# Raw weights of the first four steps in eight large buffers, with the order of their splits and squares fixed

## The chip, the cores and the metric

The kernel runs on one core of a Trainium2 chip. The metric is the device time of one execution in microseconds; the time before is the median of three runs, 1448.05 us (1447.67 to 1449.76).

## The reference

One layer of a hybrid decoder works on 256 prompt tokens and 8 decode tokens (264 columns together), with a model width of 2048:

```python
x = x + concat([y_rg, y_ml]) @ w_out      # RG-LRU and mLSTM groups, fed by xn @ w_in, xn = rmsnorm(x)
x = x + cross_attention(rmsnorm(x), memory keys and values)
x = x + (silu(xf @ w_gate) * (xf @ w_up)) @ w_down      # xf = rmsnorm(x)
y = rmsnorm(x)
```

The part that matters here is the very first one: `xn @ w_in`, where `rmsnorm(x, g)` is `x * rsqrt(mean(x * x) + 1e-6) * g`. All arithmetic is float32.

## The kernel before

The kernel is a list of steps. A step loads a block of weights, splits it, multiplies it on TensorE with the activations and evacuates the sum. The activations lie with the model's width on the 128 partitions (16 blocks of 128 rows, held in the tile xres) and the 264 tokens along the row.

**Products of three.** TensorE multiplies in a reduced form, fp32r. To keep float32 accuracy each operand is cut into a head, which is the value rounded to fp32r, and a remainder, which is the value minus the head. A product takes three matmuls: head by head, head of the weights by remainder of the input, and remainder of the weights by head of the input (`mm3`). The heads are made by ScalarE, the remainders by VectorE, which needs the head first.

**The first four steps.** Steps 0 to 3 take the first 512 output columns of w_in. Step q covers the input blocks 4q to 4q + 3 and adds to four PSUM banks (`first`: three named ax, one named mm), so that work can start as soon as a little of x and of the weights has landed. I call one input block of a step, against 512 columns, a **chunk**: chunks 0 to 15, four to a step, each of twelve matmuls (four banks by three products). `load_first` loads a chunk's weights, 128 partitions by 4 runs of 128 elements, 256 KB in runs of 512 bytes; two chunks share a raw buffer (`raw_half`, five buffers in all). `load_x` loads blocks of xres, mostly in pairs. `split_first` makes, chunk by chunk, the input's head and remainder (`split`, with the gain g_mix), and the weights' head (ScalarE) and remainder (VectorE), in that order. From step 4 on a step has 1024 or 2048 weights a partition, split in halves of 1024 (`split_half`).

**The norm.** The rsqrt of the mean square is applied after the product, so only the sum of squares of x is needed, and not before the evacuation of step 3. Its sum is built in acc_x: blocks 0 to 7 by eight squares on ScalarE (`sumsq`) with seven additions on VectorE, behind step 1's code; blocks 8 to 15 by `last_squares`, two squares of 1056 columns and four additions, behind step 3's. In the middle of steps 5 and 6 TensorE sums acc_x over the partitions and spreads the result.

**What sets the order.** SyncE's queue, and ScalarE's and VectorE's rows of `split_first`, are in written order. The rest is placed by a scheduler by readiness and priority, so an instruction of a later step can be placed ahead of written-out rows. One such instruction matters here: the first line of `rg_coef`, a VectorE instruction of 8 columns that reads the RG-LRU's decay from the tile vecs. It belongs to work that begins at step 7. The tile vecs holds all small vectors; its first 16 columns (g_mix) are loaded by ScalarE's queue at the start, the other 442 columns by SyncE's queue behind the weights of step 1. Each engine works its own rows strictly in order. Eight semaphores (DMAHW0 to DMAHW7) mark landings in turn, so a transfer waits until the one eight places before it has landed.

In the views below one line, L61, stands for all computing instructions, since a helper records them; they are told apart by their tiles: `B<-xres,vecs` is an input's head or remainder, `w<-raw` a weights' head, `w<-raw,w` a weights' remainder, `t<-vecs` the line of rg_coef.

Of the kernel before, what the change touches and what calls it, by code (L numbers as in the profile page):

```python
# [17 lines left out]
P = 128  # L18
# [4 lines left out]
N = T + NS  # L23
# [72 lines left out]
def layer_kernel(ctx: ExitStack, tc, xT, memT, vec, wrg, w_in, w_out, w_q, w_k, w_v, w_o,  # L96
# [112 lines left out]
    def load_first(i, c):  # L209

        if c % 2 == 0:
            raws.setdefault(i, []).append(raw_half())
        r = raws[i][c // 2][:, c % 2 * 512: c % 2 * 512 + 512]
        sp.dma_start(r.rearrange("p (n m) -> p n m", m=P),
                     steps[i][0].rearrange("p (n c m) -> p c n m", c=4, m=P)[:, c])

    def split_first(i, h):

        wh, wl = wrows(sb.tile([P, WW], F32R, tag="w", bufs=4, name=nm("w")), i)
        r = raws[i][h].rearrange("p (c m) -> p c m", m=P)  # L220
        with tc.high_priority(), in_order():
            for c in range(2):
                x, k = 4 * i + 2 * h + c, slice(4 * c, 4 * c + 4)
                split(*xn(x), xres[:, x, :], V("g_mix", x))
                st["split"] = act.activation(wh[:, k], r[:, k], AF.Copy)
                dve.tensor_sub(wl[:, k], r[:, k], wh[:, k].bitcast(F32))
        splits[i, h] = (wh, wl)

    def last_squares():

        a, b = (B([P, BW])[:, 0: 4 * N] for _ in range(2))
        for t, q in ((a, 2), (b, 3)):
            act.activation(t, xres[:, 4 * q: 4 * q + 4, :].rearrange("p c n -> p (c n)"), AF.Square)
        dve.tensor_add(a, a, b)
        dve.tensor_add(a[:, 0: 2 * N], a[:, 0: 2 * N], a[:, 2 * N:])
        dve.tensor_add(a[:, 0: N], a[:, 0: N], a[:, N: 2 * N])
        dve.tensor_add(acc_x, acc_x, a[:, 0: N])
# [769 lines left out]
    def pe_first(q):  # L1007
        def f(i):
            w = W(i)
            for c in range(4):  # L1010
                for n in range(4):
                    mm3(first[n][:, :N], w(4 * c + n), rx(4 * q + c), q + c == 0, q + c == 6)
        return f
# [436 lines left out]
    for c in range(4):  # L1450
        load_first(0, c)
        if c == 0:
            load_x(sp, 1, 2)
        elif c == 1:
            load_x(sp, 2, 4)
# [7 lines left out]
    with tc.high_priority(), in_order():  # L1463
        load_x(act, 0, 1)
        act.dma_start(vecs[:, 0:16], vec[:, 0:16])
        act.activation(warm_act, ones[:, 0:1], AF.Square)
# [5 lines left out]
    kept = ExitStack()  # L1472
    for i, (src, cols, pef, evf, need) in enumerate(steps):
# [24 lines left out]
        if i == 4:  # L1498
            kept.enter_context(tc.manual_schedule(engines={mybir.EngineType.PE}))
# [3 lines left out]
        if i == 1:  # L1503
# [146 lines left out]
```

## Time and profile before

| | |
|---|---|
| median of three runs | 1448.05 us |
| the profiled execution | 1449.42 us |
| its span, from the first to the last instruction | 1447.7 us |
| TensorE busy | 1429.4 us (99%) |
| VectorE busy | 1050.5 us (73%) |
| ScalarE busy | 796.6 us (55%) |
| mean rate of all transfers | 227 GB/s |

The busy times are shares of the span. TensorE's matmuls are pipelined, so its busy time counts stretches in which it is fed, and its idle time is what the page shows as waits. Times inside the trace count from the first instruction. The 1.7 us between the execution and its span lie around the program.

### The profile page before, as it was taken

The numbers are of one execution on the slowest core, as the hardware profiler recorded it, in microseconds if no ns is written. First come the engines' busy times: TensorE is split into PE (matmuls) and PEld (weight loads), VectorE is DVE, ScalarE is ACT, GpSimd is POOL, SyncE is SP. The second block draws the span as 40 slices with busy tenths as digits, with TensorE's granted clock in tenths as the row PEclk, the third lists the DMA queues.
The fourth block names the chain that finished last, engine by engine and source line by source line (L and its number), as shares of the span: only waits on it lengthen the run. The fifth ranks groups of instructions, "written<-read, shape, count | busy, mean of one in ns | idle before, by whom it ended". The sixth has DMA issues, their size and how long they took to land.

```text
span 1447.7 us, 29974 instructions
## 1 busy us (share of the span) xinstructions
PE 1429.4 (99%) x11979; PEld 1405.0 (97%) x11979; DVE 1050.5 (73%) x2012; ACT 796.6 (55%) x1290; POOL 127.7 (9%) x203
## 2 busy tenths in 40 slices
PE   9999999999999999999999999999999999999997
PEld 8999999999999999899999999999999999999997
DVE  7966798998899999977675656555666655556565
ACT  7678786665556666655544444434444433444474
POOL 0001220000125433310000000000000000000000
PEclk9999999999999999999999999999999999999999
DMA  9745897557799887856555555555555555555473
GB/s 286 237 174 184 292 361 281 176 180 273 280 334 370 326 301 266 339 175 213 196 191 197 195 198 195 193 200 191 198 196 191 202 190 196 197 191 200 164 241 126
DMA packets 100764, 329.17 MB, mean 227 GB/s; under 512 B 11056, under 2 KB 19936, under 8 KB 100624
## 3 DMA queue, kind: packets, MB, share of 16 engines
q1 hardware_dynamic: 84624, 272.36, 54.0%
q0 software_dynamic: 15424, 54.22, 10.2%
q8 instruction: 93, 1.52, 0.4%
q10 hardware_dynamic: 576, 0.68, 0.1%
q14 instruction: 47, 0.39, 0.1%
HBM read 314.36 MB, written 12.86 MB: 226 GB/s over the span
## 4 chain that ended last, share of the span: by engine, by line
PE 56%; DVE 1%; issue 1%; ACT 0%; POOL 0%; DVEq 0%; POOLq 0%
PE mm L61 56%; DVE B L61 1%; PE ax L61 1%; DVE dw L61 0%; DVE w L61 0%; POOL ds L1198 0%; DVE t L61 0%; ACT dw L61 0%; ACT t L61 0%; DVE ax L61 0%; ACT ds L61 0%; ACT B L61 0%; ACT rstd L61 0%; DVEq L1627 0%; DVE xres L61 0%
## 5 line engine op out<-in xcount | busy, mean ns | idle before, releaser
L61 PE MATMUL mm<-B,w 128*128 128x264 f32 (+1 forms) x10960 | 1282.0, 279 | 1.8 <-DVE w L61 1.7
L61 PEld LDWEIGHTS mm<-B,w 128*128 128x128 f32 x10960 | 1261.3, 189 | 9.9 <-DVE w L61 2.3
L61 DVE TENSOR_TENSOR w<-raw,w 128x1024 fp32r<-128x1024 f32 (+1 forms) x522 | 624.0, 1197 | 300.4 <-ACT w L61 299.7
L61 ACT ACTIVATE w<-raw 128x1024 fp32r<-128x1024 f32 (+1 forms) x522 | 534.7, 1028 | 511.1 <-PE mm L61 350.8
L61 PE MATMUL mm<-w,B 128*128 128x512 f32 x384 | 86.9, 380 | 0.0
L61 PEld LDWEIGHTS mm<-w,B 128*128 128x128 f32 x384 | 70.6, 189 | 9.7 <-DVE w L61 0.4
L1540 POOL TENSOR_TENSOR B<-B,rstd 128x264 f32<-128x264 f32 x4 | 2.8, 748 | 801.1 <-ACT rstd L61 801.1
L61 DVE TENSOR_TENSOR t<-mm,rstd 128x264 f32<-128x264 f32 x96 | 41.4, 432 | 28.5 <-PE mm L61 28.4
L61 DVE SCALAR_TENSOR_TENSOR B<-B,dw 128x256 f32<-128x256 f32 x128 | 54.9, 481 | 3.1 <-ACT dw L61 3.0
L61 DVE TENSOR_TENSOR xres<-xres,mm 128x264 f32<-128x264 f32 (+1 forms) x81 | 34.1, 423 | 24.6 <-PE mm L61 24.6
L61 DVE SCALAR_TENSOR_TENSOR dw<-B,qsm,dw 128x256 f32<-128x256 f32 x96 | 48.4, 509 | 2.3 <-ACT dw L61 1.5
L61 PE MATMUL ax<-B,B 128*128 128x256 f32 (+3 forms) x276 | 44.6, 302 | 1.8 <-DVE B L61 1.0
L1198 POOL TENSOR_TENSOR ds<-dw,ds 128x256 fp32r<-128x256 f32 x32 | 35.4, 1105 | 106.8 <-ACT ds L61 106.6
L61 PEld LDWEIGHTS ax<-B,B 128*128 128x128 f32 x276 | 37.9, 191 | 4.5 <-DVE B L61 1.6
L61 ACT ACTIVATE B<-xres,vecs 128x264 fp32r<-128x264 f32 (+1 forms) x64 | 32.2, 503 | 4.0 <-DVE xres L61 2.7
L61 ACT ACTIVATE dw<-B,qsm 128x256 f32<-128x256 f32 x32 | 16.3, 508 | 27.0 <-issue 10.7
L1187 POOL DMA_DIRECT2D B<-kcT x32 | 17.3, 542 | 139.6 <-DVE B L61 126.5
L61 ACT ACTIVATE t<-xres 128x264 f32<-128x264 f32 (+1 forms) x53 | 21.1, 408 | 14.0 <-DVE xres L61 13.9
L61 ACT ACTIVATE dw<-B,B 128x128 f32<-128x128 f32 x64 | 21.2, 392 | 12.2 <-DMA B<-scr 9.0
L61 DVE SCALAR_TENSOR_TENSOR B<-xres,vecs,B 128x264 fp32r<-128x264 f32 x48 | 23.3, 486 | 4.0 <-ACT B L61 4.0
L61 ACT ACTIVATE dw<-ax,dw 128x256 f32<-128x256 f32 x32 | 15.0, 469 | 19.2 <-DVE dw L61 18.2
L61 ACT ACTIVATE B<-t 128x264 fp32r<-128x264 f32 (+1 forms) x60 | 24.1, 409 | 2.1 <-DVE t L61 2.1
(181 smaller groups left out, 680.3 us busy)
## 6 DMA issues: line engine op xcount, KB each, us to landing
raw<-w_gu SPq DMA_DIRECT2D x176, 512.0 KB, 4.1
raw<-w_d SPq DMA_DIRECT2D x80, 512.0 KB, 3.7
raw<-w_in SPq DMA_DIRECT2D x74, 512.0 KB, 5.1
raw<-w_out SPq DMA_DIRECT2D x32, 512.0 KB, 3.7
raw<-w_q SPq DMA_DIRECT2D x32, 512.0 KB, 5.5
B<-kcT POOLq DMA_DIRECT2D x32, 512.0 KB, 8.9
B<-vcT POOLq DMA_DIRECT2D x32, 512.0 KB, 10.4
raw<-w_k SPq DMA_DIRECT2D x32, 512.0 KB, 5.0
```

The source lines that it names most:

```text
L61: return f(*a, **k)
L1187: pool_e.dma_start(kc, kcT[h, b])
L1198: pool_e.tensor_sub(ws[:, 1], acc, ws[:, 0].bitcast(F32))
L1540: e.tensor_mul(st["y"](c), st["y"](c), r)
```

## The change

Five things are changed, all in steps 0 to 3:

1. The raw weights of these steps go to eight buffers of the large pool B instead of five shared ones, and from chunk 2 on two chunks come in one transfer of 512 KB, in runs of 1 KB. The input block 1 moves from SyncE's to ScalarE's queue.
2. VectorE, not ScalarE, makes the weights' head of chunk 0 (`tensor_copy`), ahead of the input's split.
3. The squares come in four equal batches of 1056 columns (`squares(q)`): batch 0 behind step 1's code, 1 behind step 2's, 2 and 3 behind step 3's.
4. ScalarE's and VectorE's rows are in written order from the start to the end of step 3's code (`early`), and not only inside `split_first`; TensorE's are in written order from the start to step 6 (`kept`), and not only from step 4.
5. The matmuls of chunk 0 are written product by product over the four banks.

```diff
     def load_first(i, c):
+        src = steps[i][0].rearrange("p (n c m) -> p n c m", c=4, m=P)
         if c % 2 == 0:
-            raws.setdefault(i, []).append(raw_half())
-        r = raws[i][c // 2][:, c % 2 * 512: c % 2 * 512 + 512]
-        sp.dma_start(r.rearrange("p (n m) -> p n m", m=P),
-                     steps[i][0].rearrange("p (n c m) -> p c n m", c=4, m=P)[:, c])
+            raws.setdefault(i, []).append(B([P, 1024]))
+        r = raws[i][c // 2].rearrange("p (n c m) -> p n c m", c=2, m=P)
+        if i + c // 2 == 0:
+            sp.dma_start(r[:, :, c], src[:, :, c])
+        elif c % 2:
+            sp.dma_start(r, src[:, :, c - 1: c + 1])
...
-        with tc.high_priority(), in_order():
+        with tc.high_priority():
             for c in range(2):
                 x, k = 4 * i + 2 * h + c, slice(4 * c, 4 * c + 4)
+                if x == 0:
+                    dve.tensor_copy(wh[:, k], r[:, :, c])
                 split(*xn(x), xres[:, x, :], V("g_mix", x))
-                st["split"] = act.activation(wh[:, k], r[:, k], AF.Copy)
-                dve.tensor_sub(wl[:, k], r[:, k], wh[:, k].bitcast(F32))
+                if x > 0:
+                    st["split"] = act.activation(wh[:, k], r[:, :, c], AF.Copy)
+                dve.tensor_sub(wl[:, k], r[:, :, c], wh[:, k].bitcast(F32))
...
-    def last_squares():
+    def squares(q):
-        a, b = (B([P, BW])[:, 0: 4 * N] for _ in range(2))
-        for t, q in ((a, 2), (b, 3)):
-            act.activation(t, xres[:, 4 * q: 4 * q + 4, :].rearrange("p c n -> p (c n)"), AF.Square)
-        dve.tensor_add(a, a, b)
...
+        t = B([P, BW])[:, 0: 4 * N]
+        act.activation(t, xres[:, 4 * q: 4 * q + 4, :].rearrange("p c n -> p (c n)"), AF.Square)
+        dve.tensor_add(t[:, 0: 2 * N], t[:, 0: 2 * N], t[:, 2 * N:])
+        if q == 0:
+            dve.tensor_add(acc_x, t[:, 0: N], t[:, N: 2 * N])
+            return
+        dve.tensor_add(t[:, 0: N], t[:, 0: N], t[:, N: 2 * N])
+        dve.tensor_add(acc_x, acc_x, t[:, 0: N])
...
+                if q + c == 0:
+                    for k, l in ((0, 0), (0, 1), (1, 0)):
+                        for n in range(4):
+                            pe.matmul(by2(first[n][:, :N]), w(n)[k], turn(rx(0)[l]), start=k + l == 0, stop=False)
+                    continue
...
-        if c == 0:
-            load_x(sp, 1, 2)
-        elif c == 1:
+        if c == 1:
             load_x(sp, 2, 4)
...
-    with tc.high_priority(), in_order():
+    kept, early = ExitStack(), ExitStack()
+    kept.enter_context(tc.manual_schedule(engines={mybir.EngineType.PE}))
+    early.enter_context(in_order())
+    with tc.high_priority():
         load_x(act, 0, 1)
         act.dma_start(vecs[:, 0:16], vec[:, 0:16])
+        load_x(act, 1, 2)
...
-        if i == 1:
-            with tc.issue_after(st["split"].ins):
-                for c in range(8):
-                    sumsq(acc_x, xres[:, c, :], c == 0)
+        if 1 <= i <= 3:
+            with tc.high_priority():
+                for q in (i - 1, 3)[: 1 + i // 3]:
+                    squares(q)
         if i == 3:
-            with tc.issue_after(st["split"].ins), tc.high_priority():
-                last_squares()
+            early.close()
```

How the rows of the engines move is seen at three places. The first is VectorE's. Before, the line of rg_coef (`t_803<-vecs`) stood behind the remainder of the weights of chunk 11 (the first row), among the additions to acc_x and ahead of chunk 12's input:

```order
L61 TENSOR_TENSOR w_269<-raw_138,w_269 128x4x128 [waits DMAHW4_49,Activation_49]
L61 TENSOR_TENSOR acc_x<-acc_x,t_330 128x264 [waits Activation_49]
L61 TENSOR_TENSOR acc_x<-acc_x,t_333 128x264 [waits DVE_49,Activation_49]
L61 TENSOR_TENSOR acc_x<-acc_x,t_336 128x264 [waits DVE_49,Activation_49]
L61 SCALAR_TENSOR_TENSOR t_803<-vecs 128x8 [waits DMAHW6_49]
L61 TENSOR_TENSOR acc_x<-acc_x,t_339 128x264 [waits DVE_49,Activation_49]
L61 SCALAR_TENSOR_TENSOR B_359<-xres,vecs,B_358 128x264 [waits DMAHW5_49,Activation_49]
```

Now it stands in the middle of chunk 3. The rows are: input's and weights' remainder of chunk 2, input's remainder of chunk 3, the line of rg_coef (`t_761<-vecs`), weights' remainder of chunk 3, and the two remainders of chunk 4:

```order
L61 SCALAR_TENSOR_TENSOR B_146<-xres,vecs,B_145 128x264 [waits DMAHW5_49,Activation_49]
L61 TENSOR_TENSOR w_154<-B_120,w_154 128x4x128 [waits DMAHW6_49,Activation_49]
L61 SCALAR_TENSOR_TENSOR B_146<-xres,vecs,B_145 128x264 [waits Activation_49]
L61 SCALAR_TENSOR_TENSOR t_761<-vecs 128x8 [waits DMAHW3_49]
L61 TENSOR_TENSOR w_154<-B_120,w_154 128x4x128 [waits Activation_49]
L61 SCALAR_TENSOR_TENSOR B_165<-xres,vecs,B_164 128x264 [waits DMAHW7_49,Activation_49]
L61 TENSOR_TENSOR w_163<-B_123,w_163 128x4x128 [waits DMAHW0_49,Activation_49]
```

It moved ahead by eight chunks, and its wait for the second part of vecs (DMAHW3 is that transfer's semaphore now) moved with it.

The second place is SyncE's queue at its start. Before, from the first weights to the second part of vecs (128x442):

```order
L214 DMA raw_116<-w_in 128x4x128
L1448 DMA xres<-xT 128x264
L214 DMA raw_116<-w_in 128x4x128
L1448 DMA xres<-xT 128x528
L214 DMA raw_121<-w_in 128x4x128 x2
L1448 DMA xres<-xT 128x528 [waits DMAHW0_49]
L214 DMA raw_125<-w_in 128x4x128 [waits DMAHW1_49]
L214 DMA raw_125<-w_in 128x4x128 [waits DMAHW2_49]
L1448 DMA xres<-xT 128x528 [waits DMAHW3_49]
L214 DMA raw_129<-w_in 128x4x128 [waits DMAHW4_49]
L214 DMA raw_129<-w_in 128x4x128 [waits DMAHW5_49]
L1462 DMA vecs<-vec 128x442 [waits DMAHW6_49]
```

Now, to the same transfer (line numbers are those of the changed kernel):

```order
L216 DMA B_116<-w_in 128x4x128 x2
L1460 DMA xres<-xT 128x528
L218 DMA B_120<-w_in 128x4x256
L1460 DMA xres<-xT 128x528
L218 DMA B_123<-w_in 128x4x256 [waits DMAHW0_49]
L1460 DMA xres<-xT 128x528 [waits DMAHW1_49]
L218 DMA B_126<-w_in 128x4x256 [waits DMAHW2_49]
L1472 DMA vecs<-vec 128x442 [waits DMAHW3_49]
```

The same bytes stand ahead of vecs, less the one input block that moved to ScalarE's queue, in eight transfers instead of twelve.

The third place is TensorE at chunk 3. Before, all four banks took head by head, then input's remainder (B_150), and only then the weights' remainder:

```order
L61 MATMUL ax_109<-B_149,w_160 128x264 [waits Activation_49]
L61 MATMUL ax_110<-B_149,w_160 128x264
L61 MATMUL ax_111<-B_149,w_160 128x264
L61 MATMUL mm_112<-B_149,w_160 128x264
L61 MATMUL ax_109<-B_150,w_160 128x264 [waits DVE_49]
L61 MATMUL ax_110<-B_150,w_160 128x264
L61 MATMUL ax_111<-B_150,w_160 128x264
L61 MATMUL mm_112<-B_150,w_160 128x264
L61 MATMUL ax_109<-B_149,w_160 128x264 [waits DVE_49]
```

Now each bank takes its three products in a row:

```order
L61 MATMUL ax_109<-B_145,w_154 128x264 [waits Activation_49]
L61 MATMUL ax_109<-B_146,w_154 128x264 [waits DVE_49]
L61 MATMUL ax_109<-B_145,w_154 128x264 [waits DVE_49]
L61 MATMUL ax_110<-B_145,w_154 128x264
L61 MATMUL ax_110<-B_146,w_154 128x264
```

The wait for the weights' remainder stands at the third matmul now and stood at the ninth before. Behind step 4 the rows of all engines stand in the same sequence in both kernels.

More of the change, by code (lines that the diff above doesn't have):

```diff
@@ L217, in split_first @@
+        if i + c // 2 == 0:
+            sp.dma_start(r[:, :, c], src[:, :, c])
+        elif c % 2:
+            sp.dma_start(r, src[:, :, c - 1: c + 1])
     def split_first(i, h):
         wh, wl = wrows(sb.tile([P, WW], F32R, tag="w", bufs=4, name=nm("w")), i)
-        r = raws[i][h].rearrange("p (c m) -> p c m", m=P)
-        with tc.high_priority(), in_order():
+        r = raws[i][h].rearrange("p (n c m) -> p n c m", c=2, m=P)
+        with tc.high_priority():
             for c in range(2):
@@ L227, in split_first @@
         splits[i, h] = (wh, wl)
-    def last_squares():
-        a, b = (B([P, BW])[:, 0: 4 * N] for _ in range(2))
-        for t, q in ((a, 2), (b, 3)):
-            act.activation(t, xres[:, 4 * q: 4 * q + 4, :].rearrange("p c n -> p (c n)"), AF.Square)
-        dve.tensor_add(a, a, b)
-        dve.tensor_add(a[:, 0: 2 * N], a[:, 0: 2 * N], a[:, 2 * N:])
-        dve.tensor_add(a[:, 0: N], a[:, 0: N], a[:, N: 2 * N])
-        dve.tensor_add(acc_x, acc_x, a[:, 0: N])
+    def squares(q):
[7 more added lines that the diff above has]
+        dve.tensor_add(acc_x, acc_x, t[:, 0: N])
@@ L1010, in f @@
             for c in range(4):
+                if q + c == 0:
[3 more added lines that the diff above has]
+                    continue
                 for n in range(4):
-                    mm3(first[n][:, :N], w(4 * c + n), rx(4 * q + c), q + c == 0, q + c == 6)
+                    mm3(first[n][:, :N], w(4 * c + n), rx(4 * q + c), False, q + c == 6)
         return f
@@ L1471, in layer_kernel @@
     pend = []
-    kept = ExitStack()
     for i, (src, cols, pef, evf, need) in enumerate(steps):
@@ L1497, in layer_kernel @@
             split_half(i + LS, 1)
-        if i == 4:
-            kept.enter_context(tc.manual_schedule(engines={mybir.EngineType.PE}))
         ps = pef(i)
```

## The prediction

> **What bounds the kernel now.** I read the page first, then the waits of TensorE, then the timeline of the first 45 us, because the change touches nothing behind that. The page's first part says that TensorE (PE) is the bound:
>
> ```profile
> PE 1429.4 (99%) x11979; PEld 1405.0 (97%) x11979; DVE 1050.5 (73%) x2012; ACT 796.6 (55%) x1290; POOL 127.7 (9%) x203
> 31.00:1434.00 1403.00, 1397.69 (x11732) 1374.51 (x11731) 1022.11 (x1949) 769.14 (x1232) 121.81 (x181) 1.00 0.64 226
> ```
>
> The second row is from the view of windows: span of the window, its length, then busy time of PE, weight load, VectorE (DVE), ScalarE (ACT) and GpSimd, the granted clock, the DMA share and GB/s. From 31 us on PE is idle for 5.3 us of 1403. The order of instructions there is the same in both kernels, so a shift of PE at 31 us should arrive at the end nearly whole. What the change can win or lose lies in steps 0 to 3, the first 30 us.
>
> There I follow PE by chunks: a chunk is 128 input rows against 512 columns, twelve matmuls in one run, four chunks to a step.
>
> ```profile
> 1.13 3.78 PE L61 MATMUL mm<-ones 128*128 128x128 f32 x16 [1.13 <-DVE pad L61]
> 5.22 1.18 PE L61 MATMUL ax<-B,w 128*128 128x264 f32 x6 [0.31 <-ACT w L61]
> 6.68 0.63 ACT L61 ACTIVATE w<-raw 128x512 fp32r<-128x512 f32 x1 [1.11 <-DMA raw<-w_in]
> 7.37 0.61 PE L61 MATMUL ax<-B,w 128*128 128x264 f32 x3 [0.30 <-ACT w L61]
> ...
> 14.40 0.84 PE L61 MATMUL ax<-B,w 128*128 128x264 f32 x6
> 17.10 0.84 PE L61 MATMUL ax<-B,w 128*128 128x264 f32 x6
> ...
> 21.22 1.98 ACT L61 ACTIVATE t<-xres 128x264 f32<-128x264 f32 x6
> 23.51 0.61 ACT L61 ACTIVATE w<-raw 128x512 fp32r<-128x512 f32 x1
> 24.17 0.60 PE L61 MATMUL ax<-B,w 128*128 128x264 f32 x3 [1.50 <-ACT w L61]
> ...
> 29.84 0.61 PE L61 MATMUL mm<-B,w 128*128 128x264 f32 x3
> ```
>
> The columns are start, duration, engine, line, operation, tiles, and in brackets the idle time and what ended it. The rows at 14.40 and 17.10 stand two chunks apart: 2.70 us, so **1.35 us a chunk** and 0.1125 a matmul. Chunk 0 starts at 5.22 and step 4 at 29.84, 24.6 us for sixteen chunks that need 21.6. The 3.0 us lost are: chunk 1, which waits at 6.68 for its weights and starts at 7.37 where 6.57 was possible (0.8); chunk 12 at 24.17, behind ScalarE's squares (1.5 idle, 1.8 against the beat); the rest in small pieces. So if everything the change aims at came for nothing, it could win about 3.0 us here and 0.3 ahead of the first matmul.
>
> **The change, part by part.** *What I look at first is not in the diff.* The rows of VectorE show that the change moved an instruction of a much later step: the copy of the decay vector `t<-vecs` (first line of rg_coef), which needs the second part of vecs. It stood behind chunk 11; now it stands between the input's remainder of chunk 3 and the weights' remainder of chunk 3. VectorE works in order, so all its work behind that row waits until the second part of vecs has landed: first the weights' remainder of chunk 3, then everything of chunks 4 to 15. PE's order is fixed now, and the third matmul of chunk 3 needs that remainder.
>
> ```profile
> 8.96 0.96 SPq L1462 DMA_DIRECT2D vecs<-vec  x1
> vecs<-vec SPq DMA_DIRECT2D x1, 221.0 KB, 5.6
> 14.63 0.41 ACT L61 ACTIVATE gbias<-vecs 4x1 f32<-4x1 f32 x2
> 23.08 0.16 DVE L61 SCALAR_TENSOR_TENSOR t<-vecs 128x8 f32<-128x8 f32 x1
> ```
>
> Before, that transfer was issued at 8.96, landed 5.6 us later, at **14.56**, and its first reader on ScalarE began at 14.63. VectorE read it at 23.08, long after. In the change its place in SyncE's queue is the same: behind the weights of chunks 0 to 7 and the inputs 1 to 7. The queue is never empty there (DMA share over 1 below), so it lands when the bytes ahead of it have passed. An earlier issue doesn't help; only faster packets do.
>
> ```profile
> 6.00:14.00 8.00, 7.70 (x67) 7.40 (x66) 5.85 (x12) 6.20 (x12) 0.00 (x0) 1.00 1.11 332
> 24.00:26.00 2.00, 1.83 (x15) 1.83 (x16) 2.00 (x6) 2.00 (x7) 0.00 (x0) 1.00 1.01 401
> 15.28 0.52 ACT L61 ACTIVATE B<-xres,vecs 128x264 fp32r<-128x264 f32 x1 [0.24 <-DMA xres<-xT]
> 16.27 0.63 ACT L61 ACTIVATE w<-raw 128x512 fp32r<-128x512 f32 x1 [0.48 <-DMA raw<-w_in]
> ```
>
> *Transfers of two chunks.* They halve the number of weight packets, from 512 bytes to 1 KB each. What 1 KB packets cost the trace doesn't show, so I bound it. An input pair lands at 15.28 and the next chunk's weights at 16.27: 0.99 us for 256 KB in 512-byte packets. Three double transfers (chunks 2 to 7) lie ahead of vecs; six times 0.99 is 5.9 us. At the 401 GB/s that the window at 24 shows, where 4 KB packets run, their 1.57 MB take 3.9 us. So vecs lands between 0 and 2.0 us earlier. From 512 bytes to 4 KB are three doublings, and 1 KB is the first of them: I take a third, 0.67, and vecs lands at **13.9**. A loss I leave out, since no packet gets smaller and no byte is added. [...]
>
> *From there to step 4.* The wait ends at 13.9; `t<-vecs` takes 0.16, the remainder 0.69 (row at 9.89 below), and PE starts some 0.05 after it: PE goes on at 14.8. Ten matmuls of chunk 3 are left, 1.1 us, and twelve chunks at 1.35, 16.2: step 4 starts at 14.8 + 1.1 + 16.2 = **32.1**, against 29.84. That is **2.3 us later**. It holds if PE runs without another wait, so I check the two engines that feed it.
>
> ```profile
> 9.48 0.49 DVE L61 SCALAR_TENSOR_TENSOR B<-xres,vecs,B 128x264 fp32r<-128x264 f32 x1
> 9.89 0.68 DVE L61 TENSOR_TENSOR w<-raw,w 128x512 fp32r<-128x512 f32 x1
> 10.49 0.48 DVE L61 SCALAR_TENSOR_TENSOR B<-xres,vecs,B 128x264 fp32r<-128x264 f32 x1
> ...
> 29.11 2.04 ACT L61 ACTIVATE B<-xres 128x1056 f32<-128x1056 f32 x2
> 32.48 0.71 DVE L61 TENSOR_TENSOR B<-B 128x528 f32<-128x528 f32 x1
> 35.72 0.43 DVE L61 TENSOR_TENSOR acc_x<-acc_x,B 128x264 f32<-128x264 f32 x1
> 38.28 0.72 PE L61 MATMUL ax<-ones,acc_x 128*128 128x1 f32 x6
> ```
>
> VectorE does a chunk in 1.01 us (9.48 to 10.49) against PE's 1.35, so after the wait it gains a third of a microsecond on PE with each chunk; for chunk 4 it is about 0.3 ahead. ScalarE does not stand behind VectorE's row: its weights' heads wait only for transfers and for freed buffers, and by 13.9 it is some three chunks ahead.
>
> *Squares.* Eight squares of 0.41 us on ScalarE and their seven additions go, and two of 1056 columns become four, one batch each behind chunks 11 and 15 and two between steps 4 and 5. The first costs ScalarE 1.0 us after chunk 11, when it is over four chunks ahead: hidden by that lead. On VectorE the batches cost 0.71 + 0.43 (first), then 0.71 + 0.43 + 0.43 each, 5.8 us in all; the first two, 2.7 us, fall ahead of step 4, where the lead after twelve chunks is over 4 us. The last addition to acc_x comes near 36 us, and the sums over it, at 38.28 before, now come near 40.5. Nothing waits. The 1.5 us that chunk 12 lost to the squares are gone, but PE no longer arrives there early enough to use it.
>
> *First chunk.* VectorE's copy of the first piece takes the place of ScalarE's (0.61) ahead of the first matmul; the copy in that form is not in the trace. Between 0.3 us, half of ScalarE's time, and the 0.69 of the subtraction, I take 0.5. PE can't start before the 3.78 us of warm-up matmuls from 1.13 are done, at 4.91, so at most 0.3 us are won at the start. Chunk 1's input moves to ScalarE's queue, so the second piece is issued one place earlier on SyncE. All of it ends in the wait at chunk 3 and is worth **nothing**: chunk 3 waits for a transfer, whatever PE did before.
>
> *Pairs and buffers.* Chunk 2 now lands with chunk 3, and its third matmul needs VectorE's remainder 0.7 us after the head; before, eight matmuls came ahead of it, now two. That costs about 1 us at chunk 2, and it too lies inside the wait. The eight buffers from the pool B free the five raw buffers for steps 4 to 6 earlier; PE ran from 24.17 to 29.84 in 5.7 us for four chunks, so it had hardly waited for those.
>
> **Sum.** The profiled execution took 1449.42 us with a span of 1447.7; with +2.3 it gives 1451.7. The median of the runs, 1448.05, is 1.4 lower, and the forecast stands on it: **1450.3**. Bounds of the packet rate: no gain gives vecs at 14.56 and +2.9, 1451.0; the full 2.0 gives +0.9, 1449.0.
>
> **Rivals.**
>
> *The clock falls in the new idle stretch: slower.* PE would be idle from about 11.5 (chunk 2 lands near 8.8, its remainder is there at 10.1, ten matmuls, two of chunk 3) to 14.8, over 3 us in one piece. Before, the longest was 1.5 us, and the granted clock stayed at 1.00 through it:
>
> ```profile
> 20.00:25.00 5.00, 3.50 (x31) 3.30 (x30) 4.17 (x12) 4.63 (x13) 0.00 (x0) 1.00 1.11 344
> core 0: 1447.7 us, clock 0.998
> ```
>
> The mean clock of 0.998 says that 0.002 of 1447.7, 2.9 us, was withheld somewhere in the run. If as much is withheld again after the stretch, the time is 1450.3 + 2.9 = 1453.2. It decides once the stretch is longer than what the clock tolerates, which no row here shows beyond 1.5 us. [...] I give it 0.14.
>
> *The wait is not binding: the change does what it is meant to.* If vecs landed before 10.5, chunk 3 would follow chunk 2 at about 11.3, and thirteen chunks at 1.35 end at 28.8, 1.0 us ahead of 29.84: 1447.0. Against it stands the place of vecs at the end of 3.4 MB, which at 332 GB/s take 10.3 us by themselves, and nothing is issued ahead of 0.8. I give it 0.10. Even then the chunks 1 to 3 keep most of their loss, since weights and remainder come late.
>
> *The shift is absorbed, or grows, later.* PE's 5.3 us of waits behind 31 us follow, as far as I see, chains that start at PE, so I expect neither: 0.04 on each side, some 1448 or 1453.
>
> **Chances.** Forecast 0.68, clock 0.14, no binding wait 0.10, the last 0.04 and 0.04. About 0.2% (2.9 us) is what a measurement of this kernel can tell from no change; the runs shown spread over 2.1 us. Faster by more needs 1445.1, which even the good rival misses: 0.03. Slower by more needs 1451.0 or over: the clock, the growing shift and the forecast's upper edge, 0.10 of its 0.68: 0.28. Within: 0.69. The range leaves out the good rival and the far end of the bad one: 1448.7 to 1452.8.
>
> **What would show it.** Right: VectorE has one wait of over 3 us, on DMA vecs, ahead of a 128x8 row near 14; PE's longest wait is about 3.2 us in chunk 3, put down to VectorE's w; after it no wait of PE over 0.3 us until step 4, which starts near 32.1; ScalarE's four squares of 1056 columns end no wait. Wrong: a DVE row on vecs that starts before 11, step 4 before 30.8 or after 32.8, or a granted clock below 0.997. The packet estimate is wrong if vecs lands outside 13.4 to 14.4. The claim that a shift stays whole is wrong if step 4 and the end move by different amounts.

## The result, and the profile after

The changed kernel takes **1451.89 us** (median of 21 runs, 1449.74 to 1454.76) against 1449.44 for the kernel before (21 runs): a ratio of 1.0020, 95% interval 1.0014 to 1.0025. It is slower by 2.45 us by the medians, at the 0.2% (2.9 us) that the prediction named as the least it could tell from no change. The profiled execution took 1450.36 us with a span of 1448.6, one of the shortest of the 21; why that matters comes out below.

First the waits of VectorE in the first 40 us, then those of TensorE (PE) in the first 60; the columns are the total, how often, and the longest:

```profile
DVE t L61 <- DMA vecs<-vec: 3.3, 1, 3.3
DVE w L61 <- DMA B<-w_in: 3.2, 1, 3.2
...
PE ax L61 <- DVE w L61: 3.3, 3, 2.8
PE mm L61 <- DVE pad L61: 1.1, 1, 1.1
```

VectorE waits once for vecs. PE waits three times for one of VectorE's remainders, once of them for long, 2.8 us. The timeline shows both long waits, with the first matmul and the issue of vecs:

```profile
4.25 0.43 DVE L61 CAST w<-B 128x512 fp32r<-128x512 f32 x1 [3.18 <-DMA B<-w_in]
4.85 1.03 PE L61 MATMUL ax<-B,w 128*128 128x264 f32 x3
6.25 0.56 SPq L1472 DMA_DIRECT2D vecs<-vec  x1
...
11.00 0.39 PE L61 MATMUL ax<-B,w 128*128 128x264 f32 x2
13.40 0.17 DVE L61 SCALAR_TENSOR_TENSOR t<-vecs 128x8 f32<-128x8 f32 x1 [3.27 <-DMA vecs<-vec]
13.48 0.68 DVE L61 TENSOR_TENSOR w<-B,w 128x512 fp32r<-128x512 f32 x1
14.22 1.05 PE L61 MATMUL ax<-B,w 128*128 128x264 f32 x7 [2.83 <-DVE w L61]
...
19.31 1.07 ACT L61 ACTIVATE B<-xres 128x1056 f32<-128x1056 f32 x1
31.31 0.95 PE L61 MATMUL mm<-B,w 128*128 128x264 f32 x7
```

PE stops after two matmuls of chunk 3 and goes on at 14.22. From there it runs without a gap: the first three matmuls of the last row end step 3, so its last matmul starts at 31.31 + 2 x 0.1125 = 31.54. Before, the row at 29.84 began with that same matmul. Step 3 ends 1.70 us later. Clock in this execution, by windows of 3.41 us around the stretch (length, busy times of PE, weight load, VectorE, ScalarE, GpSimd, then the granted clock):

```profile
9.76:13.18 3.42, 1.62 (x12) 1.42 (x12) 0.36 (x1) 2.91 (x7) 0.00 (x0) 1.00 1.07 367
13.18:16.59 3.41, 2.37 (x21) 2.37 (x22) 3.19 (x8) 3.01 (x9) 0.00 (x0) 1.00 1.09 364
```

It stayed at 1.00 here. But 15 of the 21 runs have a mean clock of 0.997 or 0.996, and their median is 1452.58 against 1450.6 for the others; this profile is one of the six at 0.998.

### The profile page after: what moved, and what is told of

Read it like the earlier page. It is cut to its first block, busy times and chain, and to the rows that moved or that the text cites. A ratio compares the mean times of both kernels' runs of the same rounds, so it can differ in the third digit from the quotient of the medians.

```text
span 1448.6 us, 29947 instructions
## 1 busy us (share of the span) xinstructions
PE 1429.3 (99%) x11979; PEld 1405.7 (97%) x11979; DVE 1049.4 (72%) x2013; ACT 796.1 (55%) x1283; POOL 129.5 (9%) x203
## 4 chain that ended last, share of the span: by engine, by line
PE 56%; DVE 1%; issue 1%; POOL 0%; DMA 0%; ACT 0%; DVEq 0%; POOLq 0%; ACTq 0%
PE mm L61 56%; PE ax L61 1%; DVE B L61 1%; DVE dw L61 0%; DMA o_k<-t 0%; DVE w L61 0%; DVE t L61 0%; POOL ds L1210 0%; POOL B L1264 0%; ACT B L61 0%; POOL o_v L1308 0%; ACT t L61 0%; DVE ax L61 0%; ACT ds L61 0%; ACT rstd L61 0%
## 5 line engine op out<-in xcount | busy, mean ns | idle before, releaser
L61 DVE TENSOR_TENSOR w<-raw,w 128x1024 fp32r<-128x1024 f32 (+1 forms) x506 | 613.9, 1216 | 297.0 <-ACT w L61 296.2
L61 ACT ACTIVATE w<-raw 128x1024 fp32r<-128x1024 f32 (+1 forms) x506 | 525.4, 1041 | 516.8 <-PE mm L61 359.5
L61 ACT ACTIVATE t<-xres 128x264 f32<-128x264 f32 (+1 forms) x46 | 18.7, 408 | 14.0 <-DVE xres L61 13.9
L61 ACT ACTIVATE dw<-ax,dw 128x256 f32<-128x256 f32 x32 | 15.0, 469 | 18.1 <-DVE dw L61 15.7
L61 PE MATMUL ax<-B,w 128*128 128x264 f32 x144 | 20.7, 286 | 3.3 <-DVE w L61 3.3
```

Source lines behind the costliest of these rows:

```text
L61: return f(*a, **k)
```

## The experiments

Ratios are against the kernel before on the same chip (its medians there: 1448.55 to 1449.72).

### Is it the row's wait? The late row

The row is held back until VectorE's remainder of a later step's weights:

```diff
-            dve.tensor_sub(wl[:, :nch], r[:, :nch], wh[:, :nch].bitcast(F32))
+            st["rest"] = dve.tensor_sub(wl[:, :nch], r[:, :nch], wh[:, :nch].bitcast(F32))
...
-        dve.scalar_tensor_tensor(n_, lam, -1.0, lam, op0=OP.mult, op1=OP.min)
+        with tc.issue_after(st["rest"].ins):
+            dve.scalar_tensor_tensor(n_, lam, -1.0, lam, op0=OP.mult, op1=OP.min)
```

> The changed kernel, with one row moved: VectorE's first line of rg_coef (t<-vecs, 128x8) is held back until a later step's remainder has been issued, so that it no longer stands inside chunk 3. All else of the change stays. Theory (the row's wait for vecs is the whole loss): VectorE no longer waits near 13.4, the weights' remainder of chunk 3 comes at once, PE's idle 3.1 us in chunk 3 falls to some tenths. Chunks 1 to 3 keep small losses because two chunks land together; the last matmul of step 3, at 31.5 in the changed kernel and 29.8 in the one before, then starts at 28.0 to 28.9. Time 2.7 to 3.5 us below the changed kernel and 0.3 to 1.3 us below the kernel before, about 1448.6 by their medians of 1451.89 and 1449.44. Rival 1 (the pairs are the loss: the input and weights of two chunks land too late, and the row only stands where VectorE would have waited anyway): PE still idles about 2 to 3 us in chunks 2 and 3, then put down to transfers or to ScalarE, and the time stays within 1 us of the changed kernel. Rival 2 (part of the loss lies behind step 4, in another placement of later work or in the clock): step 3's end moves back by 3 us but the time by less than 2.

1447.75 us, 0.9991 (0.9983 to 1.0000): 4.1 us below the changed kernel, and level with the kernel before or a little below it. The row now stands at 43.30, and PE's timeline at chunks 2 and 3 reads:

```profile
9.89 0.49 PE L61 MATMUL ax<-B,w 128*128 128x264 f32 x2 [0.69 <-ACT w L61]
10.62 1.05 PE L61 MATMUL ax<-B,w 128*128 128x264 f32 x7 [0.23 <-DVE w L61]
11.51 0.50 PE L61 MATMUL mm<-B,w 128*128 128x264 f32 x3
11.85 1.18 PE L61 MATMUL ax<-B,w 128*128 128x264 f32 x9
...
29.06 2.19 PE L61 MATMUL mm<-B,w 128*128 128x264 f32 x18
```

The long wait is gone. Step 3's last matmul starts at 29.29, 2.25 earlier than in the changed kernel, though 0.4 later than I expected: the pair of chunks 2 and 3 lands late enough to cost 0.69. The time fell by more than the 2.25; part of the loss was something else.

### The row in its place, its data early

The row is held behind chunk 2's remainder, so that it stays in chunk 3, and ScalarE's queue loads its 8 columns early (the lines that hold the row are left out here):

```diff
-            sp.dma_start(vecs[:, 16:], vec[:, 16:])
+            o = _V["lam"][0]
+            sp.dma_start(vecs[:, 16: o], vec[:, 16: o])
+            sp.dma_start(vecs[:, o + 8:], vec[:, o + 8:])
...
+        act.dma_start(V("lam", 0, 8), vec[:, _V["lam"][0]: _V["lam"][0] + 8])
```

> The changed kernel with VectorE's row t<-vecs kept where it is, in the middle of chunk 3 (one place earlier), but with its data there early: the 8 columns of vecs that it reads are loaded by ScalarE's queue behind input block 1, and SyncE loads the rest of vecs where it did. Only the wait goes, not the row. Theory (it is the wait, not the place): as for the late row, VectorE has no wait over 1 us there, step 3's last matmul starts at 28.0 to 28.9, and the time is 2.7 to 3.5 us below the changed kernel, within 0.5 us of the kernel with the late row. One small transfer more in the first 5 us may cost up to 0.3. Rival 1 (the row itself or its place in the order disturbs VectorE and ScalarE): the time stays near the changed kernel's 1451.9. Rival 2 (the pairs): as for the late row, no gain over 1 us, PE idle in chunks 2 and 3 put down to transfers.

1447.56 us, 0.9987 (0.9978 to 0.9996). The row stands in chunk 3 and waits for nothing:

```profile
9.64 0.16 DVE L61 SCALAR_TENSOR_TENSOR t<-vecs 128x8 f32<-128x8 f32 x1
9.78 1.05 PE L61 MATMUL ax<-B,w 128*128 128x264 f32 x7 [0.23 <-DVE w L61]
```

The two kernels agree within 0.2 us. So the wait is the loss, not the row and not its place.

### The squares alone

The kernel before with the four batches of squares in place of its eight squares and two batches.

> The kernel before with one part of the change alone: the squares in four batches of 1056 columns, in place of eight single ones and two batches. Raw buffers, transfers, first piece and matmul order stay as before. My prediction put the loss of the old squares at chunk 12 (1.5 us idle, 1.8 against the beat). Theory: that stall goes, since a batch of 1.0 us stands where ScalarE is chunks ahead; step 3's last matmul starts at 28.0 instead of 29.8 and the time falls by about 1.8 us. Rival 1 (ScalarE's batch at another place makes a new stall of its own): PE idles 0.5 to 1 us behind the first or the second batch and the gain is under 1 us. Rival 2 (what is won in the first 30 us is lost in a later wait): step 3 ends 1.8 us earlier, the time falls by less than 0.8. In this kernel the row t<-vecs may stand near chunk 7; by the theory it waits until 14.5 and costs PE at most 0.5 there, since PE reaches chunk 7 at about 15.2.

1448.13 us, 0.9991 (0.9982 to 1.0000). PE's wait of 1.50 us at chunk 12 is gone, and step 3's last matmul starts at 28.36 instead of 29.84. The time fell by 1.0 us, between the theory's 1.8 and the rival's 0.8. The squares are a part of the change that pays by itself, though the interval reaches to no change; the other parts were not run alone. In the changed kernel this gain is buried under the wait.

### A longer wait, and its control

The row is written out in chunk 3, and vecs's second part is issued behind the weights of step 2:

```diff
+                if x == 3:
+                    st["n_"] = const.tile([P, 8], F32, name="lamneg")
+                    lam = V("lam", 0, 8)
+                    dve.scalar_tensor_tensor(st["n_"], lam, -1.0, lam, op0=OP.mult, op1=OP.min)
...
-        if i == 1:
+        if i == 2:
```

> The changed kernel with the wait made longer: the row on vecs stays in chunk 3, and the second part of vecs is issued behind the weights of step 2 instead of step 1, so four inputs and four chunks of weights, 1.59 MB more, stand ahead of it. At the 1.49 us per 512 KB that pairs of weights took in the changed kernel this is 4.3 to 4.6 us. Theory: vecs lands at 17.7 to 18.0 instead of 13.37, PE's idle stretch in chunk 3 grows from 3.1 to about 7.4 us, step 3's last matmul starts near 35.9 instead of 31.5, and the time is 4.3 us (3.6 to 5.0) above the changed kernel, some 1456. Rival 1 (the clock: an idle stretch of over 7 us lets the granted clock fall): as above plus up to 2.9 us, 1458 to 1459, with a granted clock under 1.00 in the windows behind the stretch. Rival 2 (slack elsewhere takes up a delay): the time rises by less than 3. Rival 3 (the row on vecs is not what chunk 3 waits for): the time rises by under 1.

1460.38 us, 1.0073 (1.0060 to 1.0086), 4 us more than the theory gave. The stretch is as long as expected, but look at the matmuls behind it, and at the clock in windows of 3.41 us, where it stands behind the five busy times:

```profile
11.52 0.39 PE L61 MATMUL ax<-B,w 128*128 128x264 f32 x2
19.01 1.91 PE L61 MATMUL ax<-B,w 128*128 128x264 f32 x7 [7.11 <-DVE w L61]
20.71 0.87 PE L61 MATMUL mm<-B,w 128*128 128x264 f32 x3
...
11.83:15.24 3.41, 0.08 (x1) 0.00 (x0) 0.00 (x0) 2.72 (x6) 0.00 (x0) 1.00 1.08 366
15.24:18.65 3.41, 0.00 (x0) 0.00 (x0) 0.46 (x2) 0.39 (x2) 0.00 (x0) 0.50 1.09 366
18.65:22.06 3.41, 3.05 (x14) 3.05 (x15) 3.41 (x8) 2.92 (x8) 0.00 (x0) 0.50 1.08 372
22.06:25.48 3.42, 3.42 (x32) 3.42 (x32) 3.42 (x8) 3.35 (x7) 0.10 (x1) 1.00 1.03 412
```

Seven matmuls take from 19.01 to 20.71, 0.22 us each after the first, where 0.1125 is the beat. The clock falls to one half at 15.24 and comes back at 22.06. PE worked 3.05 us at half speed and so lost some 1.5 us by it, an estimate: half of that time.

> Control for the kernel with the late vecs: the same placing of the row that reads vecs (written out in chunk 3, its result in a tile of its own), but vecs's second part is issued where the changed kernel issues it. The order of later work may differ a little from the changed kernel's. Theory (the dose alone made the late kernel slower): stretch of 3.1 us as in the changed kernel, step 3's last matmul at 31.5 and the time within 1.0 us of the changed kernel's 1451.9. Rival (the other later order costs by itself): step 3 ends at 31.5 as well, but the time is 1.5 to 3 us above 1451.9, and PE has more small waits between 120 and 280 us, as the late kernel's profile does.

The control took 1455.58 us, 1.0046 (1.0034 to 1.0059); the changed kernel took 1452.82 beside it. Its theory fell, its rival held: the other way of writing the row changed the order of later work, and that costs by itself (1454.18 against 1450.75 in their profiled executions, both with a mean clock of 0.998). Four of the control's five runs have a mean clock of 0.997 or 0.995, so its median holds a loss of clock as well. Waits of PE from 100 to 300 us, the control's first, then those of the changed kernel's first profile:

```profile
PE mm L61 <- DVE w L61: 3.2, 6, 0.9
PE ax L61 <- ACT B L61: 2.5, 1, 2.5
PE mm L61 <- ACT B L61: 0.9, 1, 0.9
```

```profile
PE ax L61 <- DVE B L61: 1.9, 3, 0.9
PE mm L61 <- DVE w L61: 1.7, 2, 1.5
PE ax L61 <- ACT B L61: 1.2, 1, 1.2
```

So the dose is read from the late kernel against its control: 4.80 us by the medians, or 3.9 if each is measured by its own ratio, for a vecs that lands 4.48 us later (18.17 against 13.69 in their profiles). Each ratio is known to some 0.0013, 1.9 us. This agrees with about a microsecond of time for one of wait but doesn't fix it: in the profiles step 3's last matmul starts 5.95 us later, 1.5 of it by the clock, and the medians mix wait and clock.

### Does the clock cost the changed kernel too?

Six runs go with this. The changed kernel again, as partner of the runs beside it:

> The changed kernel, nothing altered, as the partner of the runs with filled idle time, and for a second profiled execution. In its first profile the clock stayed at 1.00 through the 3.1 us stretch, yet in 15 of its 21 runs the mean clock was 0.997 or 0.996, against 6 of 21 and 4 of 27 such runs at most for the kernel before and the kernel with the late row, and these runs are the long ones. In the kernel with the late vecs the clock went to 0.50 at 15.24, 3.4 us after PE had run out of work at 11.85, and came back at 22.1. Theory (clock in part of the executions): median 1451.9 again, more than half of the runs at a clock of 0.997 or less; if the profile falls on one of these, a window near 14 to 21 us shows a clock of 0.50 with matmuls of chunk 3 at 0.22 us instead of 0.11, and step 3 ends 1 to 2 us later than 31.5. Rival (scatter that has nothing to do with the stretch): the profile of such a run shows the low clock elsewhere.

(The counts in it are partly wrong: the kernel before had four of 27 runs at 0.997 in that comparison, the late row none of eleven. Over all comparisons the kernel before has seven of 68 at 0.997, at 1448.84 to 1450.04 us, no longer than its others; a single 0.997 is no proof of a loss, the share of such runs is what counts.) 1452.82 us, 1.0022 (1.0012 to 1.0033); six of eight runs at 0.997, but again not the profiled one, whose vecs landed at 14.01 and whose step 3 ended at 32.17 at full clock.

Now the idle time is filled, and only that: `warm(10)` issues ten matmuls of ones by ones ahead of chunk 3, which the trace counts as twenty.

```diff
+                if q == 0 and c == 3:
+                    warm(10)
                 for n in range(4):
                     mm3(first[n][:, :N], w(4 * c + n), rx(4 * q + c), False, q + c == 6)
```

> The changed kernel with ten further matmuls of ones by ones (128x128, the kind that warms TensorE up at the start, 0.213 us each) between chunk 2 and chunk 3; their result is not used. They fill 2.1 of PE's 3.1 idle us; the row's wait stays, and chunk 3's third matmul still starts when vecs has landed, near 14.2. Theory (the wait costs 1.7 us at step 3's end, and the clock costs the rest of the 2.45 us in part of the executions): step 3's last matmul at 31.5 again, but no run falls to a clock of 0.996, few to 0.997, and the median is 0.5 to 1.2 us below the unaltered changed kernel: 1450.7 to 1451.4. Rival 1 (no clock loss): median as the unaltered kernel within 0.3, and as many runs at 0.997 or 0.996. Rival 2 (the fill delays chunk 3): step 3's end later than 31.8 and the time higher.

1451.48 us, 1.0013 (1.0005 to 1.0022), 1.3 below its partner; **none** of eleven runs is below 0.998. VectorE's wait for vecs is still 3.2 us, and step 3 ends at 32.17, as in the partner's profile. In its window no 3 us are idle any more:

```profile
11.00:14.00 3.00, 3.00 (x29) 3.00 (x28) 0.00 (x0) 2.56 (x7) 0.00 (x0) 1.00 1.08 370
```

The same with `warm(30)` in the late kernel:

> The kernel with the late vecs (idle stretch of 7.4 us, clock at 0.50 from 15.24 to 22.1, 1460.4 us) with thirty matmuls of ones by ones between chunk 2 and chunk 3, 6.4 us of fill whose result is not used. The wait for vecs is as long. Theory: the clock stays at 1.00 in every window from 10 to 40 us, chunk 3's matmuls take 0.11 us each instead of 0.22, step 3's last matmul starts near 36.0 instead of 37.6, and the time falls by about 1.5 us, to 1458.9; mean clock 0.998 in the runs where it was 0.995. Rival 1 (the low clock is not caused by idle time): no change within 0.5 us. Rival 2 (more of the late kernel's 8.5 us over the changed kernel came from the clock than one profile shows): the time falls by 3 us or more.

1458.16 us, 1.0062 (1.0049 to 1.0075). The clock is at 1.00 in all windows from 10 to 26 us and from 30 to 40, and step 3's last matmul starts at 36.61 where the late kernel had 37.80, although vecs landed 0.28 later. The time fell by 2.2 us, or by 1.6 if each is measured by its own ratio. Three of its five runs are still at 0.997 or 0.996; it has the control's order with a wait near 180 us (2.5 us in the control's profile, 2.1 in this one), which was not filled.

Transfers of one chunk in steps 0 and 1, the row held behind chunk 2's remainder, so that it still stands ahead of chunk 3's (the lines that hold it are left out here):

```diff
-        if i + c // 2 == 0:
-            sp.dma_start(r[:, :, c], src[:, :, c])
+        if i <= 1:
+            sp.dma_start(r[:, :, c % 2], src[:, :, c])
```

> The changed kernel with the transfers of steps 0 and 1 undone to one chunk each (512-byte runs, as before); pairs stay in steps 2 and 3. VectorE's row on vecs is held behind chunk 2's remainder, so it stays ahead of chunk 3's. First question, the packets: if their size brought vecs in at 13.37 instead of 14.56, it lands at 14.4 to 14.7 again; chunk 2 comes earlier without the pairs, PE's idle stretch runs from about 10.5 to 15.0, 4.3 us, and step 3's last matmul starts at 32.3 to 32.7 at full clock, 0.8 to 1.2 later than in the changed kernel. Rival: the queue and not the packets decides, vecs lands at 13.4. Second question, the clock: its rows in all profiles fall on a grid of 3.413 us (10240, 6827 and 1437011 ns are 3, 2 and 421 steps), and the first rise, between 4.02 and 7.29, gives each execution its phase. It fell after a step without work (late kernel, 11.83 to 15.24) and after one busy for 0.54 us (end of the kernel with the late row), not after steps busy for 1.5 and 1.6 us (the changed kernel's two profiles). Theory (a step busy for less than some 40% costs the clock; a stretch of 3.0 us meets this in most phases, one of 4.3 us in all): every run, the profiled one too, has a mean clock of 0.997 or less, a stretch at 0.50 begins between 12 and 15, and the time is 1453.5 to 1455. Rival (only a wholly idle step costs it): at most a third of the runs are low, and the median is 1452.5 to 1453.5.

1454.99 us, 1.0038 (1.0026 to 1.0050). Vecs landed at 14.36. With the paired transfers it landed between 13.32 and 14.14 in seven profiles (the late row's and the filled kernel's among them), with single ones at 14.36 here, 14.54 in the kernel before and 14.76 in the one with the squares alone. The margin to the nearest is small, but the records of the packets bear the theory out: here a packet of 512 bytes takes 29.7 ns on average between 5 and 14.3 us and one of 1 KB 47.5 ns, less than two of the small ones. The theory of the clock held: all six runs are at 0.997 or less. The profile (VectorE's row, PE's, then two windows):

```profile
14.38 0.17 DVE L61 SCALAR_TENSOR_TENSOR t<-vecs 128x8 f32<-128x8 f32 x1 [5.09 <-DMA vecs<-vec]
...
15.01 2.51 PE L61 MATMUL ax<-B,w 128*128 128x264 f32 x8 [4.07 <-DVE B L61]
...
11.62:15.03 3.41, 0.02 (x1) 0.02 (x1) 0.65 (x3) 2.98 (x8) 0.00 (x0) 1.00 1.11 344
15.03:18.45 3.42, 3.41 (x14) 3.11 (x15) 3.42 (x7) 2.37 (x6) 0.00 (x0) 0.50 1.08 365
```

Step 3's last matmul starts at 34.29: 32.6 at full clock and 1.7 for 3.41 us at half speed, by estimate.

What was missing is the changed kernel itself, unaltered, in a profile with a low clock. A third profile did not show one (its steps of the grid are busy for 1.94 and 1.88 us):

> The changed kernel a third time, for one more profiled execution. By the theory of the grid (clock lost where a step of 3.413 us is busy for less than some 40%), the phase of the first rise decides: with R its time in us, the steps end at R plus multiples of 3.413. The stretch runs from about 11.4 or 12.0 to 14.2 or 14.8. If a step covers 2.0 us or more of it, the clock is at 0.50 for one step behind it and step 3 ends 1 to 1.7 us later than 31.5; if not, as in the two profiles so far (steps 1.6 and 1.5 us busy), the clock stays at 1.00. Rival: a step with more than 2.0 us of the stretch leaves the clock at 1.00, and the low means of the other runs have another source.

One run, 1449.75 us, clock 0.998, step 3's last matmul at 31.49. The fourth did:

> The changed kernel a fourth time, for a profiled execution in another phase of the clock's grid. In the three profiles so far the steps of 3.413 us cut the stretch in the middle (1.9, 2.0 and 1.5 us of idle time in the step that covers most of it) and the clock stayed at 1.00. Theory of the grid: if a step here covers more than 2.1 us of the stretch, the clock is at 0.50 for the step behind it, matmuls of chunks 3 and 4 take 0.22 us there, step 3's last matmul starts at 32.5 or later and the execution takes 1452 or more; if it covers less, the profile looks like the three before and the time is 1450 to 1451. Rival: a step that covers more than 2.1 us leaves the clock at 1.00.

1453.50 us over eight runs, 1.0030 (1.0018 to 1.0041), all eight at 0.997 or 0.996; the profiled run took 1451.71, a little under what I expected.

```profile
11.40 0.39 PE L61 MATMUL ax<-B,w 128*128 128x264 f32 x2
14.57 1.14 PE L61 MATMUL ax<-B,w 128*128 128x264 f32 x7 [2.78 <-DVE w L61]
15.50 0.87 PE L61 MATMUL mm<-B,w 128*128 128x264 f32 x3
16.16 2.19 PE L61 MATMUL ax<-B,w 128*128 128x264 f32 x9
18.14 0.84 PE L61 MATMUL mm<-B,w 128*128 128x264 f32 x3
...
12.00:15.41 3.41, 0.84 (x7) 0.84 (x8) 1.66 (x4) 3.08 (x9) 0.00 (x0) 1.00 1.07 368
15.41:18.83 3.42, 3.42 (x18) 3.42 (x18) 3.42 (x8) 2.85 (x7) 0.00 (x0) 0.50 1.09 363
18.83:22.24 3.41, 3.41 (x32) 3.41 (x32) 3.41 (x8) 3.41 (x7) 0.10 (x1) 1.00 1.07 377
```

The wait is the same as in the first profile (2.78 against 2.83). But here a step of the clock's grid, 12.00 to 15.41, holds nearly all of it and is busy for 0.84 us only, and the next step runs at one half: eighteen matmuls where the following step has 32. Step 3's last matmul starts at 33.56, 2.02 later than in the first profile: 0.35 because vecs landed later (13.72 against 13.37), the other 1.7, half of one step, because of the clock.

### A kernel that beats both

Early data, chunks 2 and 3 in transfers of their own, all chunks product by product, squares one step later:

```diff
-        if i + c // 2 == 0:
+        if i == 0:
...
+                for k, l in ((0, 0), (0, 1), (1, 0)):
+                    for n in range(4):
+                        pe.matmul(by2(first[n][:, :N]), w(4 * c + n)[k], turn(rx(4 * q + c)[l]),
+                                  start=q + c + k + l == 0, stop=q + c + k == 7)
...
-                for q in (i - 1, 3)[: 1 + i // 3]:
+                for q in ((0,), (1, 2, 3))[i - 2]:
```

> A kernel meant to beat both: the changed kernel with the wait taken away by the early load of the 8 columns (as in the kernel with the early data), chunks 2 and 3 in transfers of their own, the matmuls of all sixteen chunks product by product over the four banks, so that the remainders are needed late, and the batches of squares one step later (batch 0 behind step 2's code, 1 to 3 behind step 3's). Theory (what is left in the kernel with the early data is three waits of 0.3 to 0.5 us in chunks 1 to 3, which the late remainders and the single transfers remove, and 0.6 us at chunk 12, behind the first batch of squares): PE has no gap over 0.4 us between 5 and step 4, step 3's last matmul starts at 27.6 to 28.4 instead of 29.35, and the time is 1446.2 to 1447.0 by that kernel's 1447.56. Rival (transfers set the pace: weights of chunks 8 to 11 land late whatever PE's order is): a gap of about 1 us opens near chunks 8 to 12, and the time stays at 1447.3 or above.

1448.18 us, 0.9987 (0.9978 to 0.9996): below both kernels, but no better than the early data alone. Step 3's last matmul starts at 28.05, as expected and 1.3 earlier than there. The time missed its theory (1446.2 to 1447.0), and the rival's gap of 1 us near chunks 8 to 12 isn't there either; two waits of 0.19 and 0.26 us stay at the start of chunks 1 and 2. Some of the gain is given back at once: three squares in one run put ScalarE's next weights' head at 31.46, and PE waits in step 4 (0.33 us).

```profile
27.76 3.01 ACT L61 ACTIVATE B<-xres 128x1056 f32<-128x1056 f32 x3
31.46 3.88 ACT L61 ACTIVATE w<-raw 128x1024 fp32r<-128x1024 f32 x4
34.35 0.72 PE L61 MATMUL mm<-B,w 128*128 128x264 f32 x4 [0.33 <-DVE w L61]
```

## Why the prediction was right, and where not

**The mechanism was right.** The moved row waits 3.27 us for vecs, PE stops in chunk 3 and nowhere else before step 4 for more than 0.3 us, and the four squares end no wait of PE. The late row and the early data take the wait away in two ways, and the medians of both end below the kernel before.

**The wait was forecast some 0.3 us too long.** The failed term is "I take a third, 0.67, and vecs lands at 13.9". In four profiles of the changed kernel vecs landed at 13.37, 14.01, 13.32 and 13.72, on average at 13.6, two of them just outside the 13.4 to 14.4 that the prediction allowed, and with single transfers at 14.36. The records of the packets give the size of the term: 29.2 ns for 512 bytes in the kernel before (5 to 14.5 us) and 47.5 ns for 1 KB in the changed one (6 to 13.3 us). For the 1.57 MB ahead of vecs on sixteen engines that is an estimated 1.05 us saved, where the prediction took 0.67. The step from there was good: row, remainder and 154 matmuls, 18.1 us from the row's start to step 3's last matmul, which is what the first profile shows (13.40 to 31.54). One slip in it: the row at 29.84 starts with step 3's last matmul and not with step 4, most of which comes 0.1 later; that is why 32.1 was to be set against 29.95.

**The clock rival was no rival but a second part, and I gave it too little.** Its place was right; the chance of 0.14 was for all executions or none. A mean clock of 0.997 or 0.996 stands in 29 of the 38 runs of the changed kernel, and in none of the eleven with the stretch filled. In the fourth profile step 4 begins at 33.67, past the 32.8 that the prediction named as a sign of being wrong. Its price, 2.9 us, came from a wrong reading: the mean clock of 0.998 is the idle end of the program, as this window of the kernel before shows, where no engine works:

```profile
1442.00:1447.00 5.00, 0.00 (x0) 0.00 (x0) 0.00 (x0) 0.00 (x0) 0.00 (x0) 0.57 0.82 309
```

The price that the fourth profile shows is half of one step of 3.41 us, 1.7. Its clock changes at 5.17, 15.41, 18.83 and 1445.60 us, 3, 1 and 418 such steps apart, and the step ahead of the one at 0.50, from 12.00 to 15.41, was not idle: it was busy for 0.84 us. The 0.14 was an estimate of mine; the rows I had then showed the clock staying at 1.00 through 1.5 us of idle time and nothing on a longer stretch between two matmuls.

**So the 2.45 us are a sum of two things.** The nine runs at 0.998 have a median of 1450.6 and the 29 others 1452.9; the kernel before took 1449.2 in the 68 runs of the comparisons that followed. The wait alone costs about 1.4 by this (1.8 by the filled kernel), and the clock about 2.3 on top in three executions of four, of which the trace of one explains 1.7; the rest is open. The sum on the profiled execution, 1451.7, came out near the 1451.89 because too much wait and no clock made up for each other, which is luck. The forecast of 1450.3 was lower only because the three runs then at hand had a median of 1448.05; in 21 runs it was 1449.44.

**That a shift at step 4 reaches the end whole** failed by the prediction's own sign: in the first profile step 3 ends 1.70 later and PE's last work 0.94 later (1439.18 against 1438.24). But the shift isn't lost soon. PE's sum over acc_x stands at 40.09 where the kernel before had 38.28, 1.81 later, and a matmul on ds, the same in both, at 443.79 against 441.71, 2.08 later. At 590 us, the kernel before first, then the changed one, 1.00 is left:

```profile
589.79 0.38 PE L61 MATMUL ax<-ds,onesr 128*128 128x256 f32 x1 [0.17 <-POOL ds L1198]
590.79 0.31 PE L61 MATMUL ax<-ds,onesr 128*128 128x256 f32 x1
```

The kernel with the squares alone, which runs ahead of the kernel before, gains there too: 0.89 ahead at 440.82, 1.82 at 587.97. That points to time which the one profiled execution of the kernel before lost there, and not to a slack that takes up a shift; with one profile of that kernel it isn't shown.

**Squares, first chunk, pairs.** PE's first matmul came 0.37 earlier (4.85 against 5.22; forecast were at most 0.3), and nothing of it was left behind chunk 3, as forecast. The squares are worth 1.0 us alone.

**Open:** the kernels without the wait end step 3 between 28.05 and 29.36, but their medians lie within 0.7 us and in another sequence; why an end of step 3 before 29.3 brings nothing more wasn't found. How much work keeps the clock can be narrowed by two steps of the grid elsewhere, one at the end of the late kernel, with the step behind it, and one of the late filled kernel, also with the step behind it:

```profile
1445.42:1448.84 3.42, 1.38 (x13) 1.19 (x11) 2.93 (x10) 1.62 (x5) 2.41 (x4) 1.00 0.40 141
1448.84:1452.25 3.41, 0.00 (x0) 0.00 (x0) 1.71 (x6) 0.00 (x0) 0.43 (x1) 0.50 1.01 376
...
181.37:184.79 3.42, 1.54 (x14) 1.34 (x12) 1.53 (x6) 3.17 (x8) 0.54 (x1) 1.00 1.00 369
184.79:188.20 3.41, 3.23 (x23) 3.07 (x24) 3.17 (x12) 3.36 (x6) 0.85 (x2) 1.00 1.02 410
```

1.38 us of work lost the clock and 1.54 kept it; each is a single step.

## What to carry to other kernels

When a change fixes the order of rows, look at what the scheduler then puts between them: one instruction of 0.16 us for a step far ahead made the matmul engine wait 2.8 us, because it stood in a strict queue in front of work that was due. Read an idle stretch of the matmul engine twice, once as its length and once against the clock (here 2.83 us of wait left it at 1.00 in one execution, and 2.78 us were followed by 3.42 us at 0.50 in another), and bring in the few columns that an early row needs in a transfer of their own. A single profile can fall into the rarer kind of execution; compare its clock with that of all runs before you explain the median from it.

## What the runs showed of the hardware

The changes of the granted clock that the profiles here show lie whole steps of 3.413 us apart: from the first rise to the fall at the end 1437.011 us, 421 steps, in the kernel before (5.73 to 1442.74) and in the changed one (6.35 to 1443.36); from 15.24 to 22.06 us, 2 steps, in the late kernel; and in the fourth profile of the changed kernel 10.24, 3.41 and 1426.77 us, 3, 1 and 418 steps, between 5.17, 15.41, 18.83 and 1445.60. The phase of this grid differs from one execution to the next: the first rise fell between 4.02 and 7.29 us. Ahead of it a 128x264 matmul took 0.22 us (5.67 to 5.89 in the changed kernel) instead of 0.1125, though the clock column shows 1.00 there.

Steps of the grid in which TensorE was busy for 0.00 us (late kernel, 15.24 to 18.65), 0.02 (single transfers), 0.08 (late kernel, 11.83 to 15.24), 0.54 (end of the late row's kernel), 0.84 (fourth profile) and 1.38 (end of the late kernel) were followed by one at 0.50; after steps busy for 1.54 (late filled kernel), 1.58 and 1.62 us (second and first profile of the changed kernel) the clock stayed at 1.00.

Packets of 512 bytes took 29.2 ns on average in the kernel before (5 to 14.5 us) and packets of 1 KB 47.5 ns in the changed one (6 to 13.3 us); with the single transfers they took 29.7 and 47.5 ns in one stretch (5 to 14.3 us). The second part of vecs landed between 13.32 and 14.01 us in four profiles of the changed kernel, a spread of 0.7 us.
